# Mixer of a hybrid decoder step: the decays of each chunk behind given high parts of weights, and rows of C asked for three products sooner

## The chip, the cores and the metric

The kernel runs on one core of one Trainium2 chip. The metric is the device time of one execution in microseconds (us), as the median of repeated runs. A core has five engines with a queue of instructions each: TensorE (PE, matrix products into PSUM), VectorE (DVE), ScalarE (ACT), GpSimd (POOL) and SyncE (SP). Here SP only issues DMA transfers, as does POOL beside some arithmetic. Each engine works its queue in order; engines wait for one another by semaphores.

## The reference

One layer of a hybrid decoder, for a prompt of 256 positions and 8 single decode steps (264 columns in all, `T`; the prompt alone is `TP`), all in fp32:

```
proj = rms_norm(x, g_mix) @ w_in                  # -> q, k, v, z, xbc, dt
attn = sliding-window attention (q, k, v)
xs, B, C = split(silu(causal_dwconv(xbc)))        # 4 groups of 8 heads, 4 groups of B and C
la    = cumsum(dt * a)                            # within chunks of 128
decay = exp(where(causal, la[l] - la[s], -inf))
cb    = einsum('bclgn,bcsgn->bclsg', C, B)
y     = einsum('bclsgh,bcsghp->bclghp', cb * decay, xs * dt)
y    += einsum('bclgn,bcghpn->bclghp', C, h_prev) * exp(la)   # state of the chunk before
x = x + concat(attn, rms_norm((y + d_skip*xs) * silu(z))) @ w_out
x = x + cross_attend(x, memory);  x = x + conv_ffn(x)
```

The prompt has two chunks of 128 positions, c = 0 and 1. For the decode steps the stored state `h0` of each head is multiplied by the row of C of that step and summed.

## The kernel before

Every weight is fp32 and is used as a high part and a low part. A *weight part* is a block of 128 x 1024: SP loads it (`wraw`, L83, four buffers), ACT casts the high part (`whi`, L89), DVE subtracts it (`wlo`, L90), four buffers each. The load of a part waits until the subtract of the part four before has freed its buffer. PE then does three products for each of eight 128 x 128 blocks (L105, L106, L107: high by high, high by low, low by high), 24 products of 128 x 264 in all. Parts are counted from 0 in the order in which they are used; #48 to #63 belong to the stretch below.

The mixer's projection runs in pairs of column blocks, two parts for each pair and half of the rows. `conv_group(g)` makes the two pairs of x of group g (g = 0 to 3) and their convolution (L765 to L774 and L779 to L789). `ssd_prompt(g)` is the chunked scan of one group. The order of the program is `conv_group(0)`, `conv_group(1)`, `ssd_prompt(0)`, `conv_group(2)`, `ssd_prompt(1)`, `conv_group(3)`, then eight `z_pair`, with `ssd_prompt(2)` and `(3)` behind the first two.

For each group `logs()` asks on SP for a tile `late`: two pieces of 512 KB (L825, the la of both chunks, broadcast to 128 partitions) and two pieces of 128 KB (L829, the `ti` quarter). ACT turns the first into decays: for each chunk eight Relu with the head's own la as bias (L847, the differences, clipped), then one Exp (L848). DVE multiplies them with C·B (L849). PE multiplies the decays with xs·dt (L877). The quarter `ti` goes through one Exp on ACT (L890) and is multiplied into the product of C with the state of chunk 0 (L888, L891). Bank `x` of PSUM, of which there is one, holds in turn the transposed xs of each chunk (read by L857 and L861) and the state products (L867); `hp` (L870) is ACT's copy of the first state, which the next state product waits for.

`ssd_sample` does the decode steps: for each (g, q) a tile `cb` of rows of C is asked for on POOL's queue (L920), then four state tiles `h0` are loaded there, multiplied (L924) and summed (L925) on DVE. They stand behind given low parts of weights (`lows[-d]`).

A scheduler of the framework fixes each engine's order before the run, from the order of the program, priorities (the loads, casts and subtracts of weights and the evacuation of products come first) and the dependencies. `tc.issue_after(i)` adds that an instruction stands behind instruction i. `marks["attn"]` is an instruction of the attention, long done in this stretch.

Of the kernel before, what the change touches and what calls it, by code (L numbers as in the profile page):

```python
# [7 lines left out]
F32 = mybir.dt.float32  # L8
F32R = mybir.dt.float32r
AF = mybir.ActivationFunctionType  # L10
ALU = mybir.AluOpType
# [37 lines left out]
def hybrid_decoder_step_kernel(ctx: ExitStack, tc: tile.TileContext, I, O):  # L49
    nc = tc.nc  # L50
    V, S, P, PE = nc.vector, nc.scalar, nc.gpsimd, nc.tensor
# [9 lines left out]
    def psum(tag):  # L61
        return ps.tile([128, 512], F32, tag=tag, name=tag, bufs=banks[tag])
# [10 lines left out]
    def raw_part(n=NPART):  # L73
        return wpool.tile([128, n], F32, tag="wraw", name="wraw", bufs=4)

    def weights(src, n=2048, into=None):

        out = []
        with tc.high_priority():
            for o in range(0, n, NPART):  # L80
                w = min(NPART, n - o)
                x = raw_part(w)
                marks["load"] = nc.sync.dma_start(out=x, in_=src[:, o:o + w])  # L83
                if into:
                    hi, lo = into
                else:
                    hi = wpool.tile([128, w], F32R, tag="whi", name="whi", bufs=WBUFS)
                    lo = wpool.tile([128, w], F32R, tag="wlo", name="wlo", bufs=WBUFS)
                S.copy(out=hi, in_=x)  # L89
                lows.append(V.tensor_tensor(out=lo, in0=x, in1=hi.bitcast(F32), op=ALU.subtract))  # L90
                out.append((hi, lo))
        return out
# [6 lines left out]
                V.scalar_tensor_tensor(out=lo, in0=x, scalar=g, in1=hi.bitcast(F32), op0=ALU.mult, op1=ALU.subtract))  # L99

    marks = {}
    lows = []

    def mm3(out, wh, wl, xh, xl, start, stop):
        PE.matmul(out, wh, xh, start=start, stop=False)  # L105
# [44 lines left out]
    op = oc.enter_context(tc.tile_pool(name="op", bufs=1))  # L150
# [118 lines left out]
    def pc(name, i=0, n=1):  # L269
        o = _PC[name][0]  # L270
        return par[:, o + i:o + i + n]
# [10 lines left out]
    def tr(out, in_):  # L282
        k = in_.shape[0]
        return PE.transpose(out, in_, cst[0:k, C_ID:C_ID + k])  # L284
# [54 lines left out]
    mp = mix.enter_context(tc.tile_pool(name="mp", bufs=1))  # L339
    dram_la = tc.dram_tile([2, 32, 128], F32, name="dram_la")  # L340
    dram_ds = tc.dram_tile([32, 16], F32, name="dram_ds")
    dram_bc = tc.dram_tile([2, 32, 128], F32, name="dram_bc")
# [6 lines left out]
    def t32(name):  # L349
        return t6[:, next(t6n), :]  # L350
# [102 lines left out]
    q = t32("q")  # L453
# [378 lines left out]
    def ssd_prompt(g):  # L832
        hs = slice(8 * g, 8 * g + 8)
        hp = mp.tile([128, 512], F32, tag="hp", name="hp", bufs=1)
        late = lates[g]
        p = psum("s")
        es, xdts = [], []
        for c in range(2):
            cs = slice(c * 128, c * 128 + 128)
            cbt = p[:, 256 * c:256 * c + 128]  # L840
            cbm = p[:, 256 * c + 128:256 * c + 256]
            PE.matmul(cbt, BT[:, g, cs], CT[:, g, cs], start=True, stop=True)
            V.tensor_tensor(out=cbm, in0=cbt, in1=tri, op=ALU.mult)
            e = late[:, 1024 * c:1024 * c + 1024].rearrange("p (h l) -> p h l", h=8)
            with tc.issue_after(marks["attn"].ins):
                for j in range(8):
                    S.activation(out=e[:, j, :], in_=e[:, j, :], func=AF.Relu, scale=-1.0, bias=la[:, c * 32 + 8 * g + j:c * 32 + 8 * g + j + 1])  # L847
                S.activation(out=e, in_=e, func=AF.Exp, scale=-1.0)  # L848
            V.tensor_tensor(out=e, in0=e, in1=cbm.unsqueeze(1).broadcast_to([128, 8, 128]), op=ALU.mult)  # L849
            es.append(e)  # L850
        sts = []
        for c in range(2):
            p = psum("x")
            for i in range(4):
                tr(p[:, i * 128:i * 128 + 128], xs[g][:, i, c * 128:c * 128 + 128])
            xdt = mp.tile([128, 8, 64], F32, tag="xdt", name="xdt", bufs=2)
            V.tensor_tensor(out=xdt, in0=p.rearrange("p (h q) -> p h q", h=8),  # L857
                            in1=dtn[:, c, hs].unsqueeze(2).broadcast_to([128, 8, 64]), op=ALU.mult)
            xdts.append(xdt)
            xw = mp.tile([128, 8, 64], F32, tag="bc", name="xw", bufs=2)  # L860
            V.tensor_tensor(out=xw, in0=p.rearrange("p (h q) -> p h q", h=8),  # L861
                            in1=de[:, c, hs].unsqueeze(2).broadcast_to([128, 8, 64]), op=ALU.mult)
            sts.append(xw)

        def state(c):
            st = psum("x")
            PE.matmul(st, Bn[:, c, g, :], sts[c].rearrange("p h q -> p (h q)"), start=True, stop=True)  # L867
            return st

        S.copy(out=hp, in_=state(0))  # L870
        for i in range(4):
            S.activation(out=xs[g][:, i, :TP], in_=xs[g][:, i, :TP], func=AF.Copy, scale=pc("d_skip", 4 * g + i))
        ys = [psum(k) for k in ("y", "s")]

        def own(c, h):
            o = (h % 2) * 64
            return PE.matmul(ys[c][o:o + 64, (h // 2) * 128:(h // 2) * 128 + 128], xdts[c][:, h, :], es[c][:, h, :], start=True, stop=True)  # L877

        with tc.issue_after(own(1, 7).ins):
            for c in range(2):  # L880
                for h in range(7 if c else 8):
                    own(c, h)
        for c in range(2):
            x = xs[g][:, :, c * 128:c * 128 + 128]
            V.tensor_tensor(out=x, in0=x, in1=ys[c].rearrange("p (i l) -> p i l", i=4), op=ALU.add)
        yi = psum("y")
        for i in range(4):
            PE.matmul(yi[:, i * 128:i * 128 + 128], hp[:, i * 128:i * 128 + 128], CT[:, g, 128:256], start=True, stop=True)  # L888
        ti = late[:, 2048:2560].rearrange("p (i l) -> p i l", i=4)
        S.activation(out=ti, in_=ti, func=AF.Exp)  # L890
        V.tensor_tensor(out=ti, in0=yi.rearrange("p (i l) -> p i l", i=4), in1=ti, op=ALU.mult)  # L891
        P.tensor_tensor(out=x, in0=x, in1=ti, op=ALU.add)
        st = state(1)
        hl = hp.rearrange("p (h q) -> p h q", h=8)
        P.tensor_tensor(out=hl, in0=hl, in1=d1[:, hs].unsqueeze(2).broadcast_to([128, 8, 64]), op=ALU.mult)
        V.tensor_tensor(out=hp, in0=hp, in1=st, op=ALU.add)
        nc.sync.dma_start(out=O["state_p"][g], in_=hp)
# [12 lines left out]
    todo = iter([(g, q, i) for g in range(4) for q in range(2) for i in range(4)])  # L910
    held = {}

    def ssd_sample(*behind):

        for d in behind:
            g, q, i = next(todo)
            rows = slice(4 * q, 4 * q + 4)
            if i == 0:
                held["cb"] = mp.tile([128, 4, 128], F32, tag="cb", name="cb", bufs=2)
                nc.gpsimd.dma_start(out=held["cb"], in_=dram_bc[1][8 * g + 4 * q:8 * g + 4 * q + 4, :].partition_broadcast(128))  # L920
            h0 = mp.tile([128, 4, 128], F32, tag="h0", name="h0", bufs=3)
            nc.gpsimd.dma_start(out=h0, in_=I["h0"][4 * g + i][:, rows, :])
            with tc.issue_after(lows[-d].ins):
                V.tensor_tensor(out=h0, in0=h0, in1=held["cb"], op=ALU.mult)  # L924
                V.tensor_reduce(out=ych[:, 4 * g + i, rows], in_=h0, op=ALU.add, axis=AX.X)  # L925

    def conv_group(g):
        for i in (0, 2):
            conv_pair(4 * g + i, xs[g][:, i:i + 2, :TP])
            ssd_sample(*([3, 1] if i else [1] if g else []))  # L930
        gs = slice(4 * g, 4 * g + 4)
        x = ysam[:, gs, :]
        conv_sample(4 * g, x)
        V.tensor_tensor(out=xds[:, gs, :], in0=x, in1=dsb[:, gs, 0:8], op=ALU.mult)
        V.tensor_tensor(out=x, in0=x, in1=pc("d_skip", 4 * g, 4).unsqueeze(2).broadcast_to([128, 4, 8]), op=ALU.mult)
# [48 lines left out]
    with tc.issue_after(marks["load"].ins):  # L984
        logs()
    ssd_prompt(0)
    conv_group(2)
    with tc.issue_after(marks["load"].ins):
        logs()
    ssd_prompt(1)  # L990
    conv_group(3)
    with tc.issue_after(marks["load"].ins):
        logs()
    nc.sync.dma_start(out=O["conv_new"], in_=cnew)
    for i in range(8):
        z_pair(i)
        ssd_sample(*([3, 1] if i in (1, 3, 5) else [1]))
        if i < 2:
            ssd_prompt(2 + i)
        if i in (3, 5, 7):  # L1000
            res_load()
# [358 lines left out]
    for u in range(1, 4):  # L1360
        with tc.issue_after(heads[0].ins), tc.issue_after(heads[1].ins):
            proj([I["w_co"][u]], [(OH, OL)], lambda m, pm, u=u: x2_ev(4 * u + m, pm), nb=4,
                 tag=[cyc[(4 * (u - 1) + m) % 5] for m in range(4)])
# [284 lines left out]
```

## Time and profile before

| | us |
|---|---|
| median of three runs | 1380.64 |
| lowest and highest | 1380.09, 1381.97 |
| the profiled execution | 1382.16 |
| its span (first to last instruction) | 1380.4 |
| granted clock of PE, mean | 0.999 of full |

The profile lists what each engine did in one execution. "Busy" is time in which an engine worked on instructions, "idle before" the time ahead of an instruction in which it had none in work, with the engine and line that ended it. An instruction's duration overlaps with the next one's start by some tenths of a us, so that a step is read from one start to the next. Times within the trace are us from the start of the span.

### The profile page before, as it was taken

To read this page: it belongs to the slowest core of one execution; us is meant where nothing else is said; L and a number is where in the kernel's file an instruction comes from. 1 tells how busy PE (TensorE), PEld (TensorE's weight loads), DVE (VectorE), ACT (ScalarE), POOL (GpSimd) and SP (SyncE) were. 2 spreads that over 40 slices of the span, in tenths; PEclk is the share of its full clock that TensorE was granted. 3 is DMA by queue.
4 is the path that set the end of the run, shared out by engine and by line. 5 is a ranking of instruction groups with operands and counts; after the bars stand their busy time and mean duration, and the time that the engine had idled before them with its cause. 6 is when DMAs were issued, how large, how long until landed. Compare 5 with 4: busy or idle time off the path is not lost.

```text
span 1380.4 us, 28658 instructions
## 1 busy us (share of the span) xinstructions
PE 1372.4 (99%) x11412; PEld 1348.3 (98%) x11412; DVE 1044.4 (76%) x1797; ACT 770.5 (56%) x1255; POOL 92.1 (7%) x284
## 2 busy tenths in 40 slices
PE   9999999999999999999999999999999999999998
PEld 8999999999999999899999999999999999999998
DVE  8889879999987774578777765776577657765655
ACT  7667686655545555565565544554455445543532
POOL 0000101111100000002010000000000000000000
PEclk9999999999999999999999999999999999999999
DMA  7954577666776566866676765676567555655654
GB/s 299 330 159 151 167 243 253 207 222 220 243 246 226 184 236 209 302 239 196 191 260 215 258 213 186 213 257 213 186 214 244 197 184 199 199 182 184 195 184 138
DMA packets 88325, 298.31 MB, mean 216 GB/s; under 512 B 11904, under 2 KB 17024, under 8 KB 87680
## 3 DMA queue, kind: packets, MB, share of 16 engines
q1 hardware_dynamic: 82688, 277.61, 60.7%
q0 software_dynamic: 5504, 18.88, 4.2%
q8 instruction: 89, 1.46, 0.4%
q14 instruction: 44, 0.36, 0.1%
HBM read 280.77 MB, written 16.23 MB: 215 GB/s over the span
## 4 chain that ended last, share of the span: by engine, by line
PE 93%; DMA 2%; ACT 2%; DVE 1%; issue 1%; SPq 0%; ACTq 0%
PE mm L106 20%; PE mm L105 20%; PE mm L107 20%; PE t L107 9%; PE t L105 9%; PE t L106 9%; DMA late<-dram_la 2%; ACT late L847 1%; PE t L246 1%; PE t L284 1%; DVE wlo L90 1%; PE mm L246 0%; PE s L246 0%; ACT whi L89 0%; PE x L867 0%
## 5 line engine op out<-in xcount | busy, mean ns | idle before, releaser
L89 ACT CAST whi<-wraw 128x1024 fp32r<-128x1024 f32 x440 | 460.0, 1048 | 508.2 <-PE mm L106 252.0
L90 DVE TENSOR_TENSOR wlo<-wraw,whi 128x1024 fp32r<-128x1024 f32 x440 | 541.4, 1232 | 224.7 <-ACT whi L89 218.7
L107 PE MATMUL t<-x2h,wlo 128*128 128x264 f32 x704 | 198.6, 282 | 0.0
L106 PE MATMUL t<-x2l,whi 128*128 128x264 f32 x704 | 198.4, 282 | 0.0
L105 PE MATMUL t<-x2h,whi 128*128 128x264 f32 x704 | 198.4, 282 | 0.0
L106 PE MATMUL mm<-hl,whi 128*128 128x264 f32 x704 | 197.6, 282 | 0.0
L107 PE MATMUL mm<-hh,wlo 128*128 128x264 f32 x704 | 197.3, 282 | 0.0
L105 PE MATMUL mm<-hh,whi 128*128 128x264 f32 x704 | 195.7, 282 | 0.0
L105 PE MATMUL mm<-x2h,whi 128*128 128x264 f32 x672 | 189.4, 282 | 0.0
L106 PE MATMUL mm<-x2l,whi 128*128 128x264 f32 x672 | 189.4, 282 | 0.0
L107 PE MATMUL mm<-x2h,wlo 128*128 128x264 f32 x672 | 189.4, 282 | 0.0
L105 PE MATMUL mm<-xh,whi 128*128 128x264 f32 x576 | 165.3, 287 | 1.5 <-DVE u L789 1.1
L106 PE MATMUL mm<-xl,whi 128*128 128x264 f32 x576 | 164.7, 286 | 0.0
L107 PE MATMUL mm<-xh,wlo 128*128 128x264 f32 x576 | 164.3, 287 | 0.0
L107 PEld LDWEIGHTS t<-x2h,wlo 128*128 128x128 f32 x704 | 131.9, 187 | 0.0
L105 PEld LDWEIGHTS t<-x2h,whi 128*128 128x128 f32 x704 | 131.9, 187 | 0.0
L106 PEld LDWEIGHTS t<-x2l,whi 128*128 128x128 f32 x704 | 131.9, 187 | 0.0
L106 PEld LDWEIGHTS mm<-hl,whi 128*128 128x128 f32 x704 | 131.9, 187 | 0.0
L107 PEld LDWEIGHTS mm<-hh,wlo 128*128 128x128 f32 x704 | 131.7, 187 | 0.0
L105 PEld LDWEIGHTS mm<-hh,whi 128*128 128x128 f32 x704 | 130.8, 187 | 0.0
L105 PEld LDWEIGHTS mm<-x2h,whi 128*128 128x128 f32 x672 | 125.9, 187 | 0.0
L106 PEld LDWEIGHTS mm<-x2l,whi 128*128 128x128 f32 x672 | 125.9, 187 | 0.0
(522 smaller groups left out, 2934.7 us busy)
## 6 DMA issues: line engine op xcount, KB each, us to landing
wraw<-in_w_up_dram SPq DMA_DIRECT2D x176, 512.0 KB, 4.3
wraw<-in_w_in_dram SPq DMA_DIRECT2D x96, 512.0 KB, 4.6
wraw<-in_w_dn_dram SPq DMA_DIRECT2D x88, 512.0 KB, 4.2
wraw<-in_w_out_dram SPq DMA_DIRECT2D x48, 512.0 KB, 4.5
h<-in_h_dram POOLq DMA_DIRECT2D x32, 256.0 KB, 4.5
hn<-in_h_dram SPq DMA_DIRECT2D x16, 512.0 KB, 4.4
out_state_s_dram<-hn POOLq DMA_DIRECT2D x16, 512.0 KB, 3.9
late<-dram_la SPq DMA_DIRECT2D x8, 512.0 KB, 7.3
```

The lines of the kernel that those rows point to most:

```text
L89: S.copy(out=hi, in_=x)
L90: lows.append(V.tensor_tensor(out=lo, in0=x, in1=hi.bitcast(F32), op=ALU.subtract))
L105: PE.matmul(out, wh, xh, start=start, stop=False)
L106: PE.matmul(out, wh, xl, start=False, stop=False)
L107: return PE.matmul(out, wl, xh, start=False, stop=stop)
L246: PE.matmul(first[c][:, :T], pre[k // 2][i][:, k % 2, c * 128:(c + 1) * 128], A[k // 8][x][:, k % 8, :], start=k + i + x == 0, stop=k == K ...
L284: return PE.transpose(out, in_, cst[0:k, C_ID:C_ID + k])
L847: S.activation(out=e[:, j, :], in_=e[:, j, :], func=AF.Relu, scale=-1.0, bias=la[:, c * 32 + 8 * g + j:c * 32 + 8 * g + j + 1])
```

## The change

```diff
-                S.copy(out=hi, in_=x)
+                highs.append(S.copy(out=hi, in_=x))
...
-    lows = []
+    lows, highs = [], []
...
             e = late[:, 1024 * c:1024 * c + 1024].rearrange("p (h l) -> p h l", h=8)
-            with tc.issue_after(marks["attn"].ins):
+            with tc.issue_after(highs[2 * c - 4].ins):
                 for j in range(8):
                     S.activation(out=e[:, j, :], in_=e[:, j, :], func=AF.Relu, scale=-1.0, bias=la[:, c * 32 + 8 * g + j:c * 32 + 8 * g + j + 1])
                 S.activation(out=e, in_=e, func=AF.Exp, scale=-1.0)
...
+    def c_rows(n):
+        held[n] = mp.tile([128, 4, 128], F32, tag="cb", name="cb", bufs=2)
+        nc.gpsimd.dma_start(out=held[n], in_=dram_bc[1][4 * n:4 * n + 4, :].partition_broadcast(128))
+
+    c_rows(0)
...
-            if i == 0:
-                held["cb"] = mp.tile([128, 4, 128], F32, tag="cb", name="cb", bufs=2)
-                nc.gpsimd.dma_start(out=held["cb"], in_=dram_bc[1][8 * g + 4 * q:8 * g + 4 * q + 4, :].partition_broadcast(128))
+            if i == 1 and 2 * g + q < 7:
+                c_rows(2 * g + q + 1)
...
-                V.tensor_tensor(out=h0, in0=h0, in1=held["cb"], op=ALU.mult)
+                V.tensor_tensor(out=h0, in0=h0, in1=held[2 * g + q], op=ALU.mult)
```

The Relus and the Exp of chunk 0 stand behind the cast of the fourth last weight part that the program has recorded when it comes to `ssd_prompt(g)`, those of chunk 1 behind the second last. L890, the Exp of `ti`, has no such rule, before or after. The rows of C of a product group are asked for at the second product of the group before instead of at their own first. Lines of the changed kernel behind L910 stand five lower.

ACT around the decays of group 1 (`late_2747`; `whi_2840` to `whi_2906` before and after are the casts of parts #48, #49, #50, #51), before:

```order
L89 CAST whi_2840<-wraw_2838 128x1024
L847 ACTIVATE late_2747<-late_2747,la_645 128x128 x16
L89 CAST whi_2846<-wraw_2844 128x1024
L890 ACTIVATE late_2747<-late_2747 128x512
L848 ACTIVATE late_2747<-late_2747 128x1024
L89 CAST whi_2900<-wraw_2898 128x1024
L848 ACTIVATE late_2747<-late_2747 128x1024
L773 ACTIVATE xs1_2143<-c_2577 128x2x256
L89 CAST whi_2906<-wraw_2904 128x1024
```

and with the change:

```order
L89 CAST whi_2840<-wraw_2838 128x1024
L89 CAST whi_2846<-wraw_2844 128x1024
L773 ACTIVATE xs1_2143<-c_2579 128x2x256
L890 ACTIVATE late_2747<-late_2747 128x512
L89 CAST whi_2900<-wraw_2898 128x1024
L89 CAST whi_2906<-wraw_2904 128x1024
L770 ACTIVATE c_2719<-u1_655,par_67 128x256 x2
L89 CAST whi_2982<-wraw_2980 128x1024
L847 ACTIVATE late_2747<-late_2747,la_645 128x128 x8
```

The sixteen Relus left their place between the casts of #48 and #49; the first eight stand behind the cast of #52 now. L890 of the same tile stayed ahead of the cast of #50, with nothing of the tile ahead of it.

ACT around `hp` of group 1 with the change (`late_3513` is group 3's tile, `whi_3369`, `whi_3423` and `whi_3429` are the casts of #61, #62 and #63):

```order
L872 ACTIVATE xs1_2143<-xs1_2143,par_67 128x256 x4
L89 CAST whi_3369<-wraw_3367 128x1024
L89 CAST whi_3423<-wraw_3421 128x1024
L890 ACTIVATE late_3513<-late_3513 128x512
L782 ACTIVATE tsm_3125<-csm_3122 128x32
L870 COPY hp_3135<-x_3179 128x512
L773 ACTIVATE xs2_2144<-c_3102 128x2x256
L89 CAST whi_3429<-wraw_3427 128x1024
```

Before, sixteen Relus and two Exps of group 3 and the casts of #62 to #64 stood ahead of `hp`; of group 3's tile only L890 does now.

SP around the loads of group 1's tile (`wraw_2898` and `wraw_2904` are the loads of #50 and #51) with the change:

```order
L83 DMA wraw_2844<-in_w_in_dram 128x1024
L83 DMA wraw_2898<-in_w_in_dram 128x1024
L825 DMA late_2747<-dram_la_432 128x1024 x2
L829 DMA late_2747<-dram_la_432 64x4x128
L83 DMA wraw_2904<-in_w_in_dram 128x1024
L829 DMA late_2747<-dram_la_432 64x4x128
L83 DMA wraw_2980<-in_w_in_dram 128x1024
```

Before, all four pieces of the tile stood between the loads of #49 and #50; they stand one part later now, the last piece two. Group 3's tile still stands right behind the load of #63, and so behind the subtract of #59.

On PE the products of `ssd_prompt(0)` and `ssd_prompt(1)` stand further ahead among the products of weight parts: L877 of group 0 seven products into part #52 (before: eight into #53), the second L867 of group 1 nineteen into #60 (before: two into #63), with L877 of group 1 sixteen into #61 (before: four into #62).

## The prediction, made before the changed kernel was run

> **What bounds the kernel now.** I read the page's busy shares first, then the table by stretches, the waits, and the timelines around them.
>
> ```profile
> PE 1372.4 (99%) x11412; PEld 1348.3 (98%) x11412; DVE 1044.4 (76%) x1797; ACT 770.5 (56%) x1255; POOL 92.1 (7%) x284
> ```
>
> TensorE (PE) is busy for 1372.4 of 1380.4 us, so at most 8.0 us lie in its gaps. The change adds and removes no product, so the time can move only by gaps and by products that run slowly. The table by stretches says where the gaps are (length, then busy time by engine, the granted clock, the DMA share).
>
> ```profile
> 190.00:210.00 20.00, 18.51 (x140) 18.09 (x139) 16.98 (x38) 16.62 (x34) 0.65 (x2) 0.91 0.76 245
> 230.00:260.00 30.00, 28.57 (x244) 27.09 (x243) 26.89 (x49) 20.31 (x39) 2.94 (x4) 1.00 0.67 206
> ```
>
> PE idles 1.5 us in 190–210, with its clock below 1.00, and 1.4 us in 230–260. Both lie in the mixer, where the edited lines run; the other 5.1 of the 8.0 us lie outside it, and the edit touches nothing there. The waits say on what.
>
> ```profile
> PE x L867 <- ACT hp L870: 1.4, 1, 1.4
> PE mm L105 <- DVE u L789: 1.1, 1, 1.1
> PE mm L105 <- ACT whi L89: 0.4, 1, 0.4
> ACT late L847 <- DMA late<-dram_la: 11.8, 5, 4.9
> ```
>
> **First stall.** The timeline of PE (start, duration, instruction, idle time before it), and two stretches:
>
> ```profile
> 200.24 0.28 PE L107 MATMUL mm<-xh,wlo 128*128 128x264 f32 x1
> 200.91 0.39 PE L105 MATMUL mm<-xh,whi 128*128 128x264 f32 x1 [0.40 <-ACT whi L89]
> 202.51 0.39 PE L105 MATMUL mm<-xh,whi 128*128 128x264 f32 x1 [1.09 <-DVE u L789]
> 203.03 0.42 PE L105 MATMUL mm<-xh,whi 128*128 128x264 f32 x1
> 206.33 0.29 PE L107 MATMUL mm<-xh,wlo 128*128 128x264 f32 x1
> 206.45 0.28 PE L105 MATMUL mm<-xh,whi 128*128 128x264 f32 x1
> 203.00:206.00 3.00, 3.00 (x16) 3.00 (x15) 3.00 (x7) 3.00 (x5) 0.00 (x0) 0.50 0.54 178
> ```
>
> At the full rate a product starts every 0.12 us (206.33 to 206.45). From 200.24 to 206.45 there are 23 steps: 2.76 us at that rate, 6.21 taken. The loss is 3.5 us, of which 1.5 is 15 products, from 203.03 to 206.33, at a granted clock of 0.50 and 0.22 us each. Who held it shows on ScalarE (ACT):
>
> ```profile
> 191.59 1.04 ACT L89 CAST whi<-wraw 128x1024 fp32r<-128x1024 f32 x1
> 194.66 2.45 ACT L847 ACTIVATE late<-late,la 128x128 f32<-128x128 f32 x8 [2.03 <-DMA late<-dram_la]
> 197.47 2.45 ACT L847 ACTIVATE late<-late,la 128x128 f32<-128x128 f32 x8 [0.36 <-DMA late<-dram_la]
> 199.82 1.03 ACT L89 CAST whi<-wraw 128x1024 fp32r<-128x1024 f32 x1
> 200.76 0.63 ACT L890 ACTIVATE late<-late 128x512 f32<-128x512 f32 x1
> ```
>
> The cast of weight part #49 (weights counted from 0, 24 products each) stands behind sixteen Relus (L847) that wait for group 1's rows, and ends at 200.76. PE needed it at 200.36.
>
> **Second stall.** PE waits at 257.24 for `hp`, a copy of a product that ACT makes late for the same sort of reason.
>
> ```profile
> 257.24 1.12 PE L867 MATMUL x<-xw,Bn 128*128 128x512 f32 x2 [1.43 <-ACT hp L870]
> 243.44 2.45 ACT L847 ACTIVATE late<-late,la 128x128 f32<-128x128 f32 x8 [4.90 <-DMA late<-dram_la]
> 256.62 0.56 ACT L870 COPY hp<-x 128x512 f32<-128x512 f32 x1
> ```
>
> The gap and the restart cost 1.6 us (1.43 idle and about 0.2 to the next start). At 243.44 ACT had stood 4.9 us on group 3's rows, ahead of three weight casts and the copy. Together **5.1 us** hang on this wait of L847.
>
> **The change, part by part.** (1) The Relus and Exps go behind casts recorded later. No instruction is added. The cast of #49 follows #48 at once, so the first stall's cause is gone: up to 3.5 us. Not gated is L890, the Exp of the last quarter of the same tile (its four rows of pieces, L829). It becomes the first instruction on ACT to meet the transfer: it stands ahead of the cast of #50 (group 1's tile) and ahead of `hp` (group 3's tile). So I ask what is late next.
>
> The transfers of group 1's tile go out behind raw part #50 now, and its last piece behind #51.
>
> ```profile
> 190.04 1.60 SPq L829 DMA_DIRECT2D late<-dram_la  x1
> 189.19 1.22 DVE L90 TENSOR_TENSOR wlo<-wraw,whi 128x1024 fp32r<-128x1024 f32 x1
> 191.22 1.23 DVE L90 TENSOR_TENSOR wlo<-wraw,whi 128x1024 fp32r<-128x1024 f32 x1
> late<-dram_la SPq DMA_DIRECT2D x8, 128.0 KB, 7.8
> DMA to landing us min/median/max: 5.7/7.7/9.6
> ```
>
> The last piece went at 190.04. Raw #50 and #51 need the buffers that the subtracts of #46 and #47 free, by 190.3 and 192.4 before; those subtracts come earlier by what ACT no longer does ahead of their casts (eight Relus fewer, 8 of 16 at 2.45 us per eight), partly given back by the Exps that remain. I take 191.6 for the last piece, between 190.0 (nothing lost) and 193.2 (the old 192.4 and 0.8 of issuing). Plus the median 7.8 us it lands at 199.4. L890 takes 0.53 (200.76 to 201.29) and the cast 0.94 (199.82 to 200.76): the high part #50 is there at **x = 200.9**.
>
> From there VectorE (DVE) sets the pace, since it has a backlog:
>
> ```profile
> 202.03 0.77 DVE L789 TENSOR_TENSOR u<-mm,r 128x264 f32<-128x264 f32 x2
> 202.72 0.29 DVE L843 TENSOR_TENSOR s<-s,cst 128x128 f32<-128x128 f32 x1
> 202.99 0.68 DVE L857 TENSOR_TENSOR xdt<-x,dtn 128x512 f32<-128x512 f32 x1
> 204.72 1.22 DVE L90 TENSOR_TENSOR wlo<-wraw,whi 128x1024 fp32r<-128x1024 f32 x1
> 215.44 1.21 DVE L849 TENSOR_TENSOR late<-late,s 128x1024 f32<-128x1024 f32 x1
> 230.68 1.12 DVE L772 SCALAR_TENSOR_TENSOR c<-u,par,c 128x256 f32<-128x256 f32 x1
> 234.13 1.21 DVE L90 TENSOR_TENSOR wlo<-wraw,whi 128x1024 fp32r<-128x1024 f32 x1
> ```
>
> The subtract of #50 began at 204.72, that of #59 ended at 235.3 (234.13 and 1.14 to the next start): 30.5 us without a gap. In the new order some 4.0 us more of work stands between the two: one decay product L849 (1.13 by the steps from start to start), two L857 and one L861 of the same shape (0.6 each), two L789 (0.69), one L843 with the small copies (0.3 to 0.4). L772, at 1.12 above, ran slowly beside POOL; I take off 0.3 for that. So #59 ends at x + 34.2 = **235.1**: DVE is given no time back there, because it started earlier and has more to do.
>
> Group 3's tile is asked for behind raw #63, which waits for that subtract.
>
> ```profile
> 238.49 0.92 SPq L829 DMA_DIRECT2D late<-dram_la  x1
> 253.09 0.23 ACT L782 ACTIVATE tsm<-csm 128x32 f32<-128x32 f32 x1
> 219.49 0.32 PE L877 MATMUL y<-late,xdt 128*64 128x128 f32 x1
> 251.00 0.32 PE L877 MATMUL y<-late,xdt 128*64 128x128 f32 x1
> 252.90 0.39 PE L107 MATMUL t<-xh,wlo 128*128 128x264 f32 x1
> ```
>
> Its last piece went 3.2 us after the subtract; with 7.8 more it lands at 235.1 + 11.0 = 246.1. Behind it on ACT are L890 0.53, L782 0.13 and `hp` 0.47 (256.62 to 257.09): `hp` is copied at **247.2**. PE's second product L867 wants it. Without stalls that row would come at 257.24 − 3.5 − 1.6 = 252.1; it now stands 55 ordinary products earlier (19 into part #60 instead of 2 into #63), 6.6 us, and the 32 products L877 of its group (251.00 to 252.90) come behind it, 2.0 us: **243.5**. PE waits there 3.7 us in sum. Earlier stalls of the same stretch don't add to this: the product cannot start before `hp`, and whatever PE lost before is already lost. One such is L877 of group 0: wanted at 219.49 − 3.5 − 25 × 0.12 = 213.0, its decays ready at x + 12.2 = 213.1 (204.72 to the end of L849 at 216.57 is 11.9, with 0.3 more work). Another is the first L867 of group 1, over a bank of PSUM that DVE frees with the second L861, about 6 us after #59; PE is there 3.1 + 0.9 us before 243.5, at 239.5, the bank at 241.
>
> Sum: −5.1 + 3.7 = **−1.4 us**.
>
> (2) The rows of C are asked for three products sooner.
>
> ```profile
> DVE h L924 <- DMA cb<-dram_bc: 1.3, 1, 1.3
> ```
>
> This wait was 1.3 us, once, on DVE, outside the stalls; PE waited for nothing there. I value it at 0, with ends of −0.3 and +0.3 us: the transfers use POOL's queue and could delay a state tile by a fraction of that wait.
>
> A rule can be weighed at the half clock, whose row (0.50 in 203–206) came after gaps of 0.6 and 1.2 us. The Trainium skill, "TensorE: Matmul & The Clock Gate", Part 1, has the clock halved after an idle window of about 3.4 us and free-running windows. The length of the slow stretch, 3.3 us, agrees with that; the gaps before it, 1.8 us in sum, are shorter than the rule says. By the rule the moved stall, if in one piece of under 3.4 us, would cost its gap alone, as in my sum.
>
> **The rivals.**
> - *All stalls go* (−5.1, 1375.5). For it: the stall rests on landings of 7.8 us, and the tile's shortest is 5.7; x would be 2.1 earlier and group 3's `hp` 4.2 earlier, at 243.0, before 243.5. Against: both transfers need it.
> - *The stall moves and halves the clock*, as 1.8 us of gaps did before: my forecast plus 1.5, 1380.7. For it: 3.7 us may come in two or three pieces (213, 239.5, 243.5). Against: a gap of 1.43 us at 257.24 was followed by a clock of 1.00.
> - *Slower: L890 holds weight casts.* It takes the Relus' place ahead of #50's cast, ungated, and everything behind it waits. The price is x + 34.2 + 12.1 − 243.5, so each us of a later landing costs one. The old sum of 5.1 is passed when the piece lands at 200.8, and +2.8 us when it lands at 203.6 (x = 205.1), which from 191.6 is 12.0 us, longer than the longest 9.6. At 204.5, with the clock halved once, 1380.6 − 5.1 + 8.8 + 1.5 = 1385.8. Two late ends together (193.2 + 9.6 = 202.8) give 7.1 of stalls, 1382.6.
> - *The change does not do what it says:* the Relus still stand ahead of casts, now those of #53 and later. There DVE's backlog hides them; I give it no chance of its own.
>
> **How the numbers follow.** The sum is against the profiled execution, 1382.16 us with a span of 1380.4. That lies 1.5 above the median of the runs, 1380.64, with the same stalls as far as one profile shows, so I subtract from the median: 1380.64 − 1.4 = **1379.2 us**. Chances: the forecast 0.58, all stalls gone 0.18, moved with half clock 0.16, slower 0.08. Range: 1375.5 (nothing left of the stalls) to 1382.0, short of the two late ends together. A difference of 0.2%, 2.8 us, is about what a measurement can tell from none. Faster by that needs at most 2.3 us of stalls left: the second case and a part of the first, 0.25. Slower is the last case, 0.08. The rest, 0.67, is within.
>
> **What would show it.** Right: no idle at 200–203 and a clock of 1.00 there; ACT waiting at L890 for the tile's transfer twice, by some us, instead of at L847; PE waiting at L867 for `hp` or `x`, around 239–247, for 3 to 4 us; the total PE busy time lower by about 1.5 where the half clock is gone. Wrong: no wait of PE in 205–260 (then landings were shorter, or the subtract of #59 ended sooner than 235), or a wait of casts #50 and #51 on L890 that PE feels at once (then the pieces went later than 193), or a new gap behind 260, where DVE was busy all the time and I assumed enough slack.

## The result and the profile after

The changed kernel takes 1385.54 us (median of seven runs) against 1380.77 for the kernel before, measured beside it: ratio 1.003, 95% interval 1.0018 to 1.0043. One of the seven runs took 6764.87 us, and the ratio leaves it out. It is **slower** by about 0.3%. The prediction, 1379.2 us with a range of 1375.5 to 1382.0, was wrong: wrong side, and outside the range. The profiled execution took 1385.11 us with a span of 1383.3, 2.9 us more than the span before. The medians lie 4 to 5 us apart, further than the spans. The profiled execution before had a stretch at half clock that cost 1.5 us; in the rounds of the experiments 40 of 63 runs of the kernel before had a mean granted clock of 1.000, which leaves no room for such a stretch, while the six other runs of the change had 0.998 or 0.999. That is a likely reason for the difference, not a shown one.

The busy shares, and the two stretches of the mixer that lost time (length, busy time of PE, PEld, DVE, ACT, POOL, granted clock, DMA share):

```profile
PE 1372.1 (99%) x11412; PEld 1348.4 (97%) x11412; DVE 1042.0 (75%) x1797; ACT 770.8 (56%) x1255; POOL 90.6 (7%) x284
170.00:190.00 20.00, 18.91 (x201) 18.06 (x201) 15.18 (x39) 13.33 (x30) 1.61 (x3) 1.00 0.78 240
190.00:210.00 20.00, 15.27 (x116) 15.06 (x115) 14.22 (x32) 9.63 (x15) 0.54 (x1) 0.91 0.75 232
230.00:260.00 30.00, 29.84 (x254) 28.36 (x253) 29.61 (x54) 18.30 (x31) 3.97 (x6) 1.00 0.75 233
```

Idle time of PE in 230–260 fell from 1.43 to 0.16 us, as was wanted of the change. In 190–210 it rose from 1.49 to 4.73, and 170–190 has a new gap of 1.1. The waits of the changed kernel between 170 and 300 us:

```profile
PE mm L105 <- DVE u L789: 4.7, 1, 4.7
PE s L739 <- DVE zz L732: 1.1, 1, 1.1
PE x L867 <- ACT hp L870: 0.2, 1, 0.2
ACT late L890 <- DMA late<-dram_la: 12.7, 4, 5.6
ACT late L847 <- DMA late<-dram_la: 3.2, 1, 3.2
```

The wait for the tiles did not go; from L847 (11.8 us before) it went to L890 (12.7 us), and 3.2 us at L847 are left, for group 0's tile. The three timelines around the long gap show the way from there to PE. ACT:

```profile
193.11 2.00 ACT L89 CAST whi<-wraw 128x1024 fp32r<-128x1024 f32 x2
197.38 0.64 ACT L773 ACTIVATE xs<-c 128x512 f32<-128x512 f32 x1 [2.27 <-DVE c L772]
203.64 0.63 ACT L890 ACTIVATE late<-late 128x512 f32<-128x512 f32 x1 [5.62 <-DMA late<-dram_la]
204.17 1.97 ACT L89 CAST whi<-wraw 128x1024 fp32r<-128x1024 f32 x2
```

DVE:

```profile
199.20 0.77 DVE L755 COPY attn<-tso 64x32 f32<-64x32 f32 x4
205.23 1.23 DVE L90 TENSOR_TENSOR wlo<-wraw,whi 128x1024 fp32r<-128x1024 f32 x1 [5.26 <-ACT whi L89]
206.38 0.77 DVE L789 TENSOR_TENSOR u<-mm,r 128x264 f32<-128x264 f32 x2
```

PE:

```profile
201.85 0.28 PE L106 MATMUL mm<-xl,whi 128*128 128x264 f32 x1
206.85 0.59 PE L105 MATMUL mm<-xh,whi 128*128 128x264 f32 x1 [4.73 <-DVE u L789]
207.24 0.42 PE L106 MATMUL mm<-xl,whi 128*128 128x264 f32 x1
210.04 0.28 PE L106 MATMUL mm<-xl,whi 128*128 128x264 f32 x1
```

The last piece of group 1's tile lands, L890 runs at 203.64, behind it the casts of parts #50 and #51. DVE stands from about 200.0 to 205.2 at the subtract of #50, and behind that subtract stand the two evacuations L789 of the pair of column blocks before. PE does not want part #50 yet (its instruction at 206.85 waits for DVE alone); it wants the bank of PSUM that the first L789 frees, and waits 4.7 us. From 206.85 to 210.04 its products go at half the clock: 14 steps take 3.19 us, at 0.12 each 1.68, so 1.5 are lost. The loss in the mixer is now 4.9 (201.85 to 206.85 less one step) + 1.5 + 1.2 (zz) + 0.2 (hp) = 7.8 us in place of 5.1: 2.7 of the 2.9 us of the span. The wait for zz is one of order: DVE copies zz (L732) at 187.20, behind the subtract of #45; before it ran at 182.78, ahead of it.

When the piece was asked for and when it landed shows in the chain of work between 172 and 207 us:

```profile
193.33 10.28 DMA late<-dram_la
```

### The profile page after: what moved, and what is told of

The parts are those of the page before. It is cut to its first block, busy times and chain, and to the rows that moved or that the text cites. A ratio compares the mean times of both kernels' runs of the same rounds, so it can differ in the third digit from the quotient of the medians.

```text
span 1383.3 us, 28658 instructions
## 1 busy us (share of the span) xinstructions
PE 1372.1 (99%) x11412; PEld 1348.4 (97%) x11412; DVE 1042.0 (75%) x1797; ACT 770.8 (56%) x1255; POOL 90.6 (7%) x284
## 4 chain that ended last, share of the span: by engine, by line
PE 95%; DMA 2%; DVE 1%; ACT 1%; issue 0%; SPq 0%; ACTq 0%
PE mm L106 20%; PE mm L105 20%; PE mm L107 20%; PE t L106 10%; PE t L107 9%; PE t L105 9%; DMA late<-dram_la 1%; PE t L246 1%; PE t L284 1%; PE x L867 0%; DMA wraw<-in_w_in_dram 0%; DVE wlo L90 0%; PE mm L246 0%; PE s L246 0%; DMA open<-in_open_dram 0%
## 5 line engine op out<-in xcount | busy, mean ns | idle before, releaser
L107 PEld LDWEIGHTS mm<-x2h,wlo 128*128 128x128 f32 x672 | 126.1, 188 | 0.0
```

What stands on the lines that cost most here:

```text
L107: return PE.matmul(out, wl, xh, start=False, stop=stop)
```

## The experiments

Times are medians in us; the ratio is to the kernel before, measured on the same chip in the same round.

| kernel | time | before beside it | ratio, 95% interval |
|---|---|---|---|
| rows of C alone | 1382.18 | 1381.47 | 0.9999, 0.9989 to 1.0009 |
| decays alone | 1385.43 | 1381.47 | 1.0026, 1.0015 to 1.0036 |
| change, L890 of group 1 gated | 1381.25 | 1381.47 | 0.9990, 0.9981 to 0.9998 |
| change, L890 of all groups gated | 1377.52 | 1381.47 | 0.9964, 0.9951 to 0.9977 |
| change, tile ahead of the load of #50 | 1383.24 | 1381.78 | 1.0013, 1.0004 to 1.0023 |
| change, evacuations ahead of the subtract | 1386.05 | 1381.78 | 1.0024, 1.0010 to 1.0037 |
| L890 of all groups gated, old rows of C | 1377.67 | 1381.78 | 0.9964, 0.9948 to 0.9979 |
| before, L890 of all groups gated | 1380.34 | 1381.58 | 0.9991, 0.9982 to 1.0000 |

My theory was: L890, the one step on the tile that was left ungated, meets the transfer first and holds the casts behind it. The rivals: the earlier rows of C crowd the tile's transfers; or the late landing costs whatever meets it.

**The two parts of the change, apart.** Rows of C alone: the changed kernel with the decays behind the attention again.

```diff
-            with tc.issue_after(highs[2 * c - 4].ins):
+            with tc.issue_after(marks["attn"].ins):
```

> Only the rows of C are asked for sooner; the decays stand behind the attention as before. Theory (the ungated Exp of ti holds the casts): the same as before within 0.1%, PE waiting for the cast of #49, for u and for hp as before, 1380 to 1382 us. Rival (the earlier rows of C crowd the transfers of the tile late): the tile lands later than before (group 1's last piece behind 201 instead of 199.3) and the time is above before, 1382 to 1385 us.

It is the same as before, at 1382.18 us (0.2 above the range that I gave); ACT waits 12.4 us for the tiles at L847, as it did, and group 1's last piece landed 8.5 us after its issue. Decays alone: the kernel before with the `highs` list and the gate, nothing else.

> Only the decays are gated; the rows of C are asked for as before. Theory: like the whole change, 1384 to 1387 us, ACT waiting some 5 us at L890 for group 1's tile and PE 4 to 5 us for u. Rival (rows of C crowd the transfers): group 1's last piece lands near 199 to 200 instead of 203.6, the wait for u is under 1.5 us, 1379 to 1381 us.

It is as slow as the whole change, with the same waits:

```profile
PE mm L105 <- DVE u L789: 5.2, 1, 5.2
PE s L739 <- DVE zz L732: 0.8, 1, 0.8
ACT late L890 <- DMA late<-dram_la: 12.4, 4, 6.1
```

The last piece of group 1 landed at 204.60. So the rows of C neither cost nor bring anything that can be measured, and the rival of crowding falls.

**One instruction.** L890 of group 1 alone goes behind the cast of part #54; on ACT nothing else changes place against the changed kernel in that stretch.

```diff
-        S.activation(out=ti, in_=ti, func=AF.Exp)
+        with tc.issue_after((highs[-2] if g == 1 else marks["attn"]).ins):
+            S.activation(out=ti, in_=ti, func=AF.Exp)
```

> The whole change, and in addition the Exp of ti (L890) of group 1 alone stands behind the cast of part #54, where its second Relus are; nothing else on ACT moves. Theory (this one instruction carries the loss): the wait of PE for u (4.7 us) and the half clock behind it (some 1.5 us) go, 1377 to 1380 us; the wait for zz of 1.1 us stays, and the wait for hp may be up to 3 us. Rival (the late landing of the tile is what costs, whoever meets it): the Relus of group 1 or the casts behind them wait instead, PE still loses 3 us or more between 195 and 215, 1382 to 1386 us.

The piece landed as late as in the changed kernel (203.3), and PE lost nothing in 190–210 us. What was behind shows now, PE's waits in 170–300 (the inserted line moves L890 to L891):

```profile
PE x L867 <- ACT hp L870: 1.4, 1, 1.4
PE y L888 <- ACT hp L870: 1.1, 1, 1.1
PE s L739 <- DVE zz L732: 0.8, 1, 0.8
PE x L284 <- DVE cnew L765: 0.4, 1, 0.4
ACT late L891 <- DMA late<-dram_la: 9.4, 3, 5.1
```

The time, 1381.25, is above the 1377 to 1380 that I had expected: I had counted one wait for `hp`, there are two. The rival falls: a late landing that nothing in front of the casts meets cost PE nothing between 190 and 210 us.

**All of them.** L890 of each group stands behind the second last high part, with the Relus of chunk 1.

```diff
-        S.activation(out=ti, in_=ti, func=AF.Exp)
+        with tc.issue_after(highs[-2].ins):
+            S.activation(out=ti, in_=ti, func=AF.Exp)
```

> The whole change, and L890 of every group stands behind the second last high part, with the Relus of chunk 1. Theory: no wait of PE for u or hp, the wait for zz under 1.1 us, 1375 to 1378 us. Rival: as in the run before, the stall goes to whatever meets the tile next, 1381 to 1386 us.

PE has no gap left in the mixer, and the whole kernel is faster than both others:

```profile
190.00:210.00 20.00, 20.00 (x170) 20.00 (x170) 19.93 (x41) 14.14 (x27) 1.08 (x2) 1.00 0.92 268
230.00:260.00 30.00, 30.00 (x257) 28.73 (x256) 28.97 (x55) 20.44 (x39) 4.26 (x5) 1.00 0.76 234
```

The last piece of group 1 took 10.8 us there, longer than in the changed kernel, and no engine noticed. With the rows of C asked for as before it is as fast:

> Decays and L890 of every group gated as in the fastest run, the rows of C asked for as before the change. Theory (the rows of C are worth nothing here): 1376.5 to 1378.5 us, no wait of PE in 170 to 300. Rival (they carry part of that gain): 1379 us or more, with a wait on DVE for cb that PE feels.

**L890 gated in the kernel before.** This fills the last corner of a square: Relus gated or not, L890 gated or not.

> The kernel before, with L890 alone gated behind the second last high part; Relus and Exps of the decays stay behind the attention. Theory (whatever meets the tile first on ACT holds the casts behind it, and here that is L847 again): PE waits 1 us or more around 200 and for hp around 255, 1380 to 1383 us. Rival (L890 is a burden of its own that the kernel before carried too): both waits shrink below 1 us, 1376 to 1379 us.

```profile
189.49 0.39 PE L105 MATMUL mm<-xh,whi 128*128 128x264 f32 x1 [1.15 <-DVE u L789]
203.02 0.39 PE L105 MATMUL mm<-xh,whi 128*128 128x264 f32 x1 [0.50 <-DVE u L789]
```

This one is split. For the theory speak the time and L847, which still stands ahead of the casts (it waited 9.9 us for the tiles). But the waits that I had named, at 1 us or more, shrank to 0.5 us for u (at 203.02) and 0.4 for `hp`, which was the rival's sign; a new wait of 1.15 us for u came at 189.49. So L890 had a share in the waits of the kernel before too. The interval ends at 1.0000, so a gain is barely told from none. The square, in ratios: neither 1, L890 alone 0.9991, Relus and Exps alone 1.0026, both 0.9964. Alone, the gate on L890 is worth 0.09%, barely told from nothing, and that on the Relus and Exps costs 0.26%; together they gain 0.36%.

**The landing.** The load of #50 goes behind the last piece again, as before the change; L890 keeps the changed kernel's place. On the other engines the order differs in one swap on ACT (L890 ahead of L773).

```diff
-                marks["load"] = nc.sync.dma_start(out=x, in_=src[:, o:o + w])
+                with tc.issue_after(marks["late"].ins) if len(lows) == 50 else ExitStack():
+                    marks["load"] = nc.sync.dma_start(out=x, in_=src[:, o:o + w])
...
-            nc.sync.dma_start(out=ti[h * 64:h * 64 + 64], in_=lav[h][4 * g:4 * g + 4, :].partition_broadcast(64))
+            marks["late"] = nc.sync.dma_start(out=ti[h * 64:h * 64 + 64], in_=lav[h][4 * g:4 * g + 4, :].partition_broadcast(64))
```

> The whole change with L890 where the change leaves it, but the load of part #50 stands behind group 1's last piece again, as before the change. Theory (the size of the loss is set by when the last piece lands): it is issued by 190 instead of 193.3 and lands near 199 instead of 203.6; the subtract of #50 ends near 201.5 and the evacuation behind it near 202, when PE wants the bank: the wait for u is under 0.8 us, with no half clock, the waits for zz (about 1) and hp (1.5 to 3.5) stay; 1380 to 1382.5 us. Rival (the place of L890 ahead of #50 costs in any case): PE waits 3 us or more for u, 1384 us or more.

The chain and PE's waits (lines stand one lower here):

```profile
191.64 8.86 DMA late<-dram_la
PE x L868 <- ACT hp L871: 1.9, 1, 1.9
PE mm L106 <- DVE u L790: 1.2, 1, 1.2
PE s L740 <- DVE zz L733: 0.8, 1, 0.8
```

The piece landed at 200.50 instead of 203.61, 3.1 us sooner, and the wait for u fell by 3.5, from 4.7 to 1.2 us: about one for one. But the piece was issued at 191.6, not by 190, and landed later than I had said; the wait is above my 0.8, and the time above my range, since a half clock follows the wait of 1.9 us for `hp` (below). In direction the theory holds, and the rival of a fixed price falls.

**The evacuations.** On DVE the subtract of #50 is put behind both L789.

```diff
-                lows.append(V.tensor_tensor(out=lo, in0=x, in1=hi.bitcast(F32), op=ALU.subtract))
+                with tc.issue_after((marks["ev"] if len(lows) == 50 else marks["load"]).ins):
+                    lows.append(V.tensor_tensor(out=lo, in0=x, in1=hi.bitcast(F32), op=ALU.subtract))
...
-        in_pair(lambda m, pm: V.tensor_tensor(out=us[:, m, 3:], in0=pm, in1=r0, op=ALU.mult))
+        in_pair(lambda m, pm: marks.update(ev=V.tensor_tensor(out=us[:, m, 3:], in0=pm, in1=r0, op=ALU.mult)))
```

> The whole change, but on DVE the subtract of #50 stands behind the two evacuations L789 of the pair before, so that they no longer queue behind a subtract that waits for its cast; the transfers and L890 stay. Theory (PE waits for a bank that DVE would have freed, not for the weights): the wait for u goes; PE wants the high part #50 near 206 and has it near 205, so at most 1 us is lost on it; with zz and hp 1380.5 to 1383 us. Rival (PE is held by the weights themselves): the wait moves to the cast or subtract of #50 at 3 us or more, 1384 to 1386 us.

Neither came out. The wait for u is gone, but not the time. PE's waits and DVE's timeline (lines stand one lower here too):

```profile
PE x L285 <- DVE xw L862: 3.3, 1, 3.3
PE x L868 <- ACT hp L871: 2.4, 2, 1.8
PE x L868 <- DVE xw L862: 1.6, 1, 1.6
PE s L740 <- DVE zz L733: 1.2, 1, 1.2
...
200.06 0.43 DVE L790 TENSOR_TENSOR u<-mm,r 128x264 f32<-128x264 f32 x1
205.48 0.48 DVE L773 SCALAR_TENSOR_TENSOR c<-u,par,c 128x256 f32<-128x256 f32 x1 [4.99 <-ACT c L771]
```

The scheduler put the first step of the convolution (L773) between the two evacuations. It needs ACT's L771, which stands behind L891 and the cast of #50 as everything on ACT does. DVE stood 5.0 us at that instruction instead of at the subtract, and PE then waited for `xw` and its bank. (PE's order differs here as well, from 206 us on, so the run is not one swap alone.) So the subtract is one of several ways by which ACT's standstill gets to PE; taking one away opens the next.

## Why the prediction was wrong

- *What bounds the kernel*: held. The only difference lies in the mixer's gaps and the half clock: 2.7 of 2.9 us.
- *The first stall's cause goes, and L890 is the first to meet group 1's transfer*: held. ACT waits at L890 for all four tiles, not for two. The second stall, for `hp`, is 0.2 us where the forecast had 3.7; the reason stands below, at the sum.
- **The step that failed is the term "191.6 + 7.8 = 199.4"**, the landing of group 1's last piece. It landed at 203.61. The issue came 1.7 us later: I let the subtracts of #46 and #47 come sooner, since fewer Relus stand ahead of their casts. They ended at about 190.1 and 192.3, as before (190.3 and 192.4). Ahead of the cast of #47 no Relu is gone: the eight of group 0's second chunk, from 187.74 on, only moved behind the cast of #46, and #47 is cast at 190.09, before at 190.14. The cast of #46 starts 0.8 us sooner, but DVE, busy with other work, came to its subtract at 188.93 (before 189.19).

```profile
187.74 2.44 ACT L847 ACTIVATE late<-late,la 128x128 f32<-128x128 f32 x8
190.09 1.03 ACT L89 CAST whi<-wraw 128x1024 fp32r<-128x1024 f32 x1
```

  The flight took 2.5 us longer: I had taken the median of all sixteen small pieces, though the trace before shows this tile's own:

```profile
late<-dram_la SPq DMA_DIRECT2D x2, 128.0 KB, 9.5
```

  That row, of the kernel before and of the two pieces issued between 189.3 and 190.2 us, gives 9.5 where I had put 7.8. With it even my own 191.6 gives a landing at 201.1, past the break-even of 200.8, and with the late issue 193.2 + 9.5 = 202.7. In the six kernels in which this piece goes behind the load of #51, it took 9.2 to 10.8 us; in the four with the old order 8.5 to 9.3.
- *The sum behind x*: held, in part by luck. It reads x + 34.2 + 12.1 − 243.5. With the measured landing x is 203.61 + 0.53 + 0.94 = 205.1 and the sum 7.9 us; 7.8 were measured. By the sum the subtract of #59 ends at 239.3 and `hp` is copied at 251.4. The changed kernel shows 239.9 and 251.3:

```profile
238.76 1.21 DVE L90 TENSOR_TENSOR wlo<-wraw,whi 128x1024 fp32r<-128x1024 f32 x1
250.22 0.63 ACT L890 ACTIVATE late<-late 128x512 f32<-128x512 f32 x1 [3.90 <-DMA late<-dram_la]
250.87 0.56 ACT L870 COPY hp<-x 128x512 f32<-128x512 f32 x1
```

  The luck is that the subtract came 0.6 us late and the last piece of group 3 flew 6.8 us, 1.0 less than 7.8. The loss did not come at `hp`, where I had put it (0.2 us), since PE had lost nearly as much before: at the evacuations behind the subtract of #50, which I had not listed among what is queued behind a waiting instruction, at the half clock behind that wait, and 1.1 us at zz. By the sum, had PE lost less there, it would have waited longer for `hp`. Waits for `hp` came back in the run in which only group 1's L890 was gated.
- *"So I subtract from the median"*: the forecast took the 5.1 us of stalls for those of the median run, 1380.64, though the profiled run, with its half clock, took 1.5 more. Most runs of the kernel before cannot have had that half clock (their clock is given with the result), so the stalls taken off were probably 1.5 us too large. There is no profile of such a run of that kernel; the rows of C alone, equal to it in time, show no half clock and 2.9 us of waits of PE. Estimate with 1.5 less: 1380.64 − 5.1 + 1.5 + 7.8 = 1384.8, where 1385.54 was measured.
- *The rows of C*: valued at 0, measured 0.9999.
- *The rivals*: "slower: L890 holds weight casts" is what happened, at the point that I had named for +2.8 us (a landing at 203.6); the spans differ by 2.9. Its chance of 0.08 was too small. I held 9.6 us for the longest flight and then asked for 12.0 in one term; it took a late issue and a long flight. I had added up these two late ends, to 1382.6 us, and left them outside the range. That they go together is not shown: issued at 194.12 in the run with the evacuations ahead, the piece flew 9.2 us; issued at 191.25 in the run with all L890 gated, it flew 10.8.

## What to carry to other kernels

When the instructions that wait for a transfer are moved out of the way, look for every other reader of the same tile on that engine: the first one left takes over the wait, and with it all that queues behind. Gate them all, or look at what is left; here the two gates gave +0.26% and −0.09% (the latter hardly told from nothing) alone and −0.36% together. Take a transfer's flight from the same transfer in the trace, at the load of that moment, and not from the median of its kind; where a sum turns on it, the range has to take in a late issue and a late end together.

## What the runs showed of the hardware

The half clock does not follow from the length of a gap. One gap of 4.73 us was followed by it (0.51 in 207–210 of the changed kernel), two of 0.40 and 1.09 us too (before), one of 1.88 us (the run with the tile ahead of the load), and one of 5.25 us (the decays alone); one of 3.34 us was not (the run with the evacuations ahead, clock 1.00 in 205–212). The changed kernel, the tile ahead of the load, the evacuations ahead, the decays alone:

```profile
207.00:210.00 3.00, 3.00 (x14) 3.00 (x15) 3.00 (x8) 1.21 (x3) 0.00 (x0) 0.51 0.59 175
224.00:227.50 3.50, 3.46 (x11) 2.54 (x12) 3.50 (x6) 2.87 (x4) 0.54 (x1) 0.56 0.38 114
205.00:212.00 7.00, 3.66 (x32) 3.48 (x31) 6.52 (x12) 7.00 (x16) 0.00 (x0) 1.00 0.35 88
205.53:212.36 6.83, 4.52 (x20) 4.52 (x21) 6.14 (x11) 4.34 (x8) 0.00 (x0) 0.50 0.27 85
```

By the records of the clock in the traces it lasted 3.41 us in three kernels and cost about 1.5; with the decays alone it lasted 6.83 and cost about 2.1. The Trainium skill, "TensorE: Matmul & The Clock Gate", Part 1, has free-running windows of about 3.4 us, one of them idle before the clock halves. The duration agrees: one window in three kernels, two in the fourth. Half clocks after gaps of 1.9 us and less do not agree with a wholly idle window.

The changes of the clock keep a grid in the traces: from the first record of the clock to the first change there are 58 steps of 3.413 us in the kernel before, 59 in the changed kernel and with the decays alone, 63 with the tile ahead of the load. But how busy PE was in the step ahead does not decide it either. That step in the kernel before, then two steps with the evacuations ahead, counted from the first record of that trace (length, then busy time of PE first):

```profile
199.49:202.90 3.41, 1.92 (x14) 1.50 (x13) 2.01 (x4) 3.41 (x6) 0.00 (x0) 1.00 0.61 241
204.27:207.69 3.42, 1.84 (x16) 1.63 (x14) 2.21 (x5) 3.42 (x5) 0.00 (x0) 1.00 0.03 12
207.69:211.10 3.41, 1.64 (x14) 1.67 (x15) 3.41 (x7) 3.41 (x11) 0.00 (x0) 1.00 0.53 159
```

Behind the first, with 1.92 us busy, the clock halved; behind the others, with 1.84 and 1.64, it did not. What decides stays open.
